# A decoder trunk on one core: split weights kept in device memory between the two halves of the tokens

## The chip, the core and the metric

The kernel runs on one core of one Trainium2 chip. The metric is device time in microseconds (us) of one execution, lower being better. The core has a matrix engine (PE, whose weight loads are listed as PEld), a vector engine (DVE), a scalar engine (ACT), a general engine (POOL), and SyncE (SP), which in this kernel issues every DMA. Each engine works through its own list of instructions in order; semaphores tie the lists together.

## The reference, cut to what matters

Two layers over 1024 tokens of width 1024. Layer 0 normalises, projects, runs a state-space mixer (S5) beside a stick-breaking attention, and projects back with `w_out`; layer 1 mixes by trailing windows. Each layer then runs a squared-ReLU MLP of width 4096 and a gated embedding:

```python
    for i in range(DEPTH):
        if i % 2 == 0:
            h = h + even_mixer(h, ln_mix_even[j], w_in_even[j], ..., w_out_even[j])
        else:
            h = h + pool_mixer(rms_norm(h, ln_mix_odd[j]), pool_w[j], pool_scale[j])
        hn = rms_norm(h, ln_mlp[i])
        h = h + jnp.square(jax.nn.relu(hn @ w_mlp_up[i])) @ w_mlp_down[i]
        gate = jax.nn.sigmoid(rms_norm(h, ln_ple[i]) @ w_ple_gate[i])
        h = h + (p[i] @ w_ple_up[i]) * gate
```

## The kernel before

**A product in three passes.** All matrices are fp32. Every operand of a large product is cut into a rounded part and a remainder (hi and lo, both fp32r), and `gemm` (L480) adds three products: hi with hi, lo with hi, hi with lo. For a weight this is done by `wload` and `split`: a DMA (L468) brings 512 KB (128 partitions x 1024 numbers) into a raw tile (tag `wr`, two buffers), ACT writes hi (L448), and DVE writes lo as raw minus hi (L452). Hi and lo are tiles of tag `wh`, eight buffers, so four pairs. In the S5 stage four of the eight hold S5 tables, in the first MLP of layer 0 four hold the hidden units; then only two pairs go round. One full weight tile feeds 24 matmuls of 128x512.

**Tokens in two halves.** A product's moving side is 512 tokens wide, so most of the program runs first for half 0 and later for half 1. Twelve tiles of `w_in` (numbered c8 to c15, then c4 to c7: keys, values, queries), four of each part of `w_out`, the first four tiles of `w_up` and of `w_down` of each layer, seven gate tiles and one `w_pu` tile of layer 0, and two tiles of `pool_w` are loaded and split once for each half: 46 tiles, twice each. The rest of the MLP is done by a seven-product scheme over both halves (`seven`), whose weights are loaded once (L882, tiles `q7`).

**What sets the order.** The source is a set of generators woven by fixed rates (`weave`): projections and `w_out` with S5 and attention, the gated embedding of layer 0 with the pooling mixer, half 0 of the next MLP with the pooling of half 1. A scheduler then lays each engine's list by priority and by when buffers come free, and adds the waits. SP's list holds, in one order, all weight loads, the loads of `x`, sets of 16 small DMAs that build S5's matrix M from `kt` (L364, four times), and the `q7` loads.

**Places that the prediction speaks of.** `put_qk` (L642) takes a projected tile out of PSUM on DVE; `s5_pass` copies `kt` on ACT (L354); `turned` copies attention weights on ACT (L735); `pool` computes windows on DVE (L1326 to L1349); `mlp` applies relu (L840), makes the hidden pair (L841 to L843) and adds into the residual (L854); `mlp_all` builds half 1's operands for the seven products on DVE (L894, L1206).

Of the kernel before, what the change touches and what calls it, by code (L numbers as in the profile page):

```python
# [11 lines left out]
F32 = mybir.dt.float32  # L12
F32R = mybir.dt.float32r
# [6 lines left out]
P = 128  # L20
# [20 lines left out]
class Kern:  # L41
    def __init__(self, ctx, tc, A):
        self.tc, self.nc, self.A = tc, tc.nc, A

        self.sb = ctx.enter_context(tc.tile_pool(name="sb", bufs=1))
        self.hi = ctx.enter_context(tc.tile_pool(name="hi", bufs=1))
        self.ps = ctx.enter_context(tc.tile_pool(name="ps", bufs=1, space=PSUM))
        self.bufs = dict(t2=3, acc=2, u=26, at=8, wq=4, r0=1, r1=1, wr=2, wh=8, mm=2, z=2, b=2, av=1, st=1)
        self.n = 0

# [410 lines left out]
            out += [(hi[:, i, :], lo[:, i, :]) for i in range(2)]  # L461
        return out

    def wload(self, src, K, tags=("wr", "wh"), hi_eng="a"):

        raw = self.t([P, 1024], tags[0], name="wr")
        hi, lo = (self.t([P, 1024], tags[1], F32R, name="w") for _ in range(2))
        self.nc.sync.dma_start(out=raw, in_=src)  # L468
        self.split(raw, hi, lo, hi_eng)
        return tuple(t.rearrange("p (k n) -> p k n", k=K) for t in (hi, lo))  # L470

    def gemm(self, ps, w, m, x, first=True, last=True, turn=0, going=False):

# [337 lines left out]
    def w_out(self, part, hf, mix, h, last=False, tag="wh"):  # L811
        for n in range(8):
            if n % 2 == 0:
                w = self.wload(self.A["w_out"][4 * part + n // 2], 4, ("wr", tag))
            ps = self.p([P, HT], "mm")
            self.gemm(ps, w, n % 2, mix)
            self.nc.vector.tensor_tensor(out=h[n], in0=h[n], in1=ps, op=ALU.add)
            if last:
                self.final(hf, n, h[n], G_MLP[0], "v")
            yield  # L820


    def mlp(self, i, f, halves, h, tag="at", up=()):

        nc, v = self.nc, self.nc.vector
        load = lambda m: self.wload(self.A["w_up"][i, 4 * f + m], 8)
        n_up = 2 if tag == "wh" else 4
        up = list(up) + [load(m) for m in range(len(up), n_up)]
        hid = {}
        for hf in halves:  # L830
            x = self.xg[hf]
            hid[hf] = self.act(4, "hid", tag)
            for m in range(4):
                ps = self.p([P, HT], "mm")
                self.gemm(ps, up[m], 0, x)
                if self.r[hf] is None:
                    self.norm_end(hf)
                hi, lo = hid[hf][m]
                t = self.t([P, HT], "t2", name="relu")
                v.scalar_tensor_tensor(out=t, in0=ps, scalar=0.0, in1=self.r[hf], op0=ALU.max, op1=ALU.mult)  # L840
                nc.scalar.activation(out=hi, in_=t, func=AF.Square)  # L841
                nc.scalar.activation(out=t, in_=t, func=AF.Square)
                v.tensor_tensor(out=lo, in0=t, in1=hi.bitcast(F32), op=ALU.subtract)  # L843
                if m + n_up < 4:
                    up.append(load(m + n_up))
                yield
        dn = None
        for hf in halves:
            for m in range(8):
                ps = self.p([P, HT], "mm")  # L850
                if m % 2 == 0:
                    dn = self.wload(self.A["w_down"][i, 4 * f + m // 2], 4)
                self.gemm(ps, dn, m % 2, hid[hf])
                v.tensor_tensor(out=h[hf][m], in0=h[hf][m], in1=ps, op=ALU.add)  # L854
                yield
# [352 lines left out]
        return x[:2], x[2:]  # L1208

    def first_up(self, i):  # L1210
        return [self.wload(self.A["w_up"][i, m], 8) for m in range(2)]

    def between(self, i, solo):

# [46 lines left out]
    def ple(self, i, halves, h):  # L1261
        nc, v = self.nc, self.nc.vector
        A = self.A
        jobs = [(m, hf) for m in range(8) for hf in halves]
        early, self.early = self.early or (None, None), None
        wu = {0: early[0] or self.wload(A["w_pu"][i, 0], 2)}
        w = {0: early[1] or self.wload(A["w_gate"][i, 0], 8)}
        ups, depth, x = [], 4, list(self.xg)

        def up(at):  # L1270
            if at < len(jobs):
                m, hf = jobs[at]
                if m // 4 not in wu:
                    wu[1] = self.wload(A["w_pu"][i, 1], 2)
                ups.append(self.p([P, HT], "zb"[at // 2 % 2]))
                self.gemm(ups[at], wu[m // 4], m % 4, self.pt[hf])

        for at in range(depth):
            up(at)
        for at, (m, hf) in enumerate(jobs):  # L1280
            if m + 1 not in w and m < 7:
                w[m + 1] = self.wload(A["w_gate"][i, m + 1], 8)
            hk = h[hf][m]
            ps = self.p([P, HT], "mm")
            self.gemm(ps, w[m], 0, x[hf], turn=4)
            if self.r[hf] is None:
                self.preload()
                self.norm_end(hf)
            sg = self.t([P, HT], "t2", name="sg")
            v.tensor_tensor(out=sg, in0=ps, in1=self.r[hf], op=ALU.mult)  # L1290
            self.last_act = nc.scalar.activation(out=sg, in_=sg, func=AF.Sigmoid)
            v.tensor_tensor(out=sg, in0=sg, in1=ups[at], op=ALU.mult)
            v.tensor_tensor(out=hk, in0=hk, in1=sg, op=ALU.add)
            up(at + depth)
            if i == 1:
                nc.sync.dma_start(out=A["out"][m, :, hf * HT:(hf + 1) * HT], in_=hk)
            else:
                self.final(hf, m, hk, G_ODD, "v", ("at", "at", "u", "u"))
            yield
        for hf in halves:  # L1300
            self.r[hf] = None


    def pool(self, hf, h):
# [7 lines left out]
        def start(m):  # L1312
            gi = m // 2
            ps = self.p([P, HT], "av")
            if m % 4 == 0:
                self.pw = self.wload(self.A["pool_w"][m // 4], 4)
            wt = [t[:, 2 * (gi % 2):2 * (gi % 2) + 2] for t in self.pw]
            self.gemm(ps, wt, m % 2, xg[2 * gi:2 * gi + 2])
            if m == 0:
                self.norm_end(hf)  # L1320
            z, nx = (self.t([P, 16 + HT], "wq", name=nm) for nm in ("pz", "win"))
            if hf == 0:
                g.memset(z[:, 0:16], 0.0)
            else:
                nc.scalar.copy(out=z[:, 0:16], in_=self.halo[:, m, :])
            v.scalar_tensor_tensor(out=z[:, 16:], in0=ps, scalar=self.gain[:, G_POOL + m:G_POOL + m + 1], in1=self.r[hf],  # L1326
                                   op0=ALU.mult, op1=ALU.mult)
            if gi == 0:
                add(v, nx[:, 16:], z[:, 16:], z[:, 15:15 + HT])
            else:  # L1330
                w = 2 << gi
                first = 0.0
                if hf == 1:
                    first = self.tail[:, m:m + 1]
                v.tensor_tensor_scan(out=nx[:, 16:], data0=z[:, 16:], data1=z[:, 16 - w:16 + HT - w], initial=first,  # L1335
                                     op0=ALU.add, op1=ALU.subtract)
            if hf == 0:
                nc.scalar.copy(out=self.halo[:, m, :], in_=z[:, HT:])
                if gi:
                    nc.scalar.copy(out=self.tail[:, m:m + 1], in_=nx[:, 15 + HT:])  # L1340
            v.tensor_tensor(out=h[m], in0=h[m], in1=z[:, 16:], op=ALU.subtract)
            win[m] = nx, z

        def finish(m):
# [5 lines left out]
            self.final(hf, m, h[m], G_MLP[1])  # L1350

        start(0)
        for m in range(8):
            if m < 7:
                start(m + 1)
            finish(m)
            yield
# [11 lines left out]
    def build(self):  # L1369
# [6 lines left out]
        s5 = chain(self.s5_params(), *(self.s5_pass(gt) for gt in range(4)))  # L1376
        self.k, self.q, self.v = [[], []], [[], []], []

        ws = self.ahead(2, [lambda c=c: self.wload(self.A["w_in"][c], 8) for _ in range(2)
                            for c in (8, 9, 10, 11, 12, 13, 14, 15, 4, 5, 6, 7)])  # L1380

        def kvq(hf):
# [42 lines left out]
        pool = self.pool(0, h[0])  # L1425
# [4 lines left out]
        pool = self.pool(1, h[1])  # L1430
# [108 lines left out]
```

## Time and profile before

| | |
|---|---|
| median of three runs | 2117.95 us (2117.68 to 2119.14) |
| the profiled execution, its own time | 2119.18 us |
| its span, first to last instruction | 2117.4 us |
| PE, DVE, ACT busy in the span | 2030.2, 1781.6, 1176.8 us |
| mean granted PE clock | 0.981 of full |
| DMA: moved, share of the 16 engines | 136.24 MB, 19.0% on the queue that SP feeds |

The span falls into stages. To about 330 us: projections with S5 woven in, then attention until 590; `w_out` of half 1 and the first MLP part of half 1 until 674; the seven products of layer 0 until about 1215; the gated embedding, the pooling mixer and layer 1's first MLP part until 1473; the seven products of layer 1 and the last gate to the end. A share of busy time is an average over all of these, so tables by stretch of time are the ones to read. A row of such a table gives, for each engine, busy microseconds and the number of instructions, then the granted clock, the share of the DMA engines and GB/s. Where a row ends in brackets, they give the idle time before the instruction and what ended it.

### The profile page before, as it was taken

The numbers are of one execution on the slowest core, as the hardware profiler recorded it, in microseconds if no ns is written. First come the engines' busy times: TensorE is split into PE (matmuls) and PEld (weight loads), VectorE is DVE, ScalarE is ACT, GpSimd is POOL, SyncE is SP. The second block draws the span as 40 slices with busy tenths as digits, with TensorE's granted clock in tenths as the row PEclk, the third lists the DMA queues.
The fourth block names the chain that finished last, engine by engine and source line by source line (L and its number), as shares of the span: only waits on it lengthen the run. The fifth ranks groups of instructions, "written<-read, shape, count | busy, mean of one in ns | idle before, by whom it ended". The sixth has DMA issues, their size and how long they took to land.

```text
span 2117.4 us, 24722 instructions
## 1 busy us (share of the span) xinstructions
PE 2030.2 (96%) x9464; PEld 1606.6 (76%) x9464; DVE 1781.6 (84%) x2339; ACT 1176.8 (56%) x1701; POOL 131.3 (6%) x263
## 2 busy tenths in 40 slices
PE   7999899999999999999999999879999999999998
PEld 5777665666677888888888887658888888888886
DVE  8876477888778798989769978988797998879999
ACT  5233478877744645555365655533654656365662
POOL 2678000000000000000000000000000000000000
PEclk9999899999999999999999999989999999999999
DMA  5121111210141210211211131231210211210221
GB/s 174 46 64 49 56 60 50 84 47 31 41 150 50 80 50 30 80 57 36 67 60 40 52 108 60 90 111 59 70 50 30 90 40 40 80 60 31 70 70 60
DMA packets 44741, 136.24 MB, mean 64 GB/s; under 512 B 9552, under 2 KB 10704, under 8 KB 44624
## 3 DMA queue, kind: packets, MB, share of 16 engines
q1 hardware_dynamic: 44624, 134.67, 19.0%
q8 instruction: 74, 1.21, 0.2%
q14 instruction: 43, 0.35, 0.1%
HBM read 129.28 MB, written 4.19 MB: 63 GB/s over the span
## 4 chain that ended last, share of the span: by engine, by line
PE 73%; DVE 18%; ACT 4%; issue 3%; DMA 1%; POOL 0%; SPq 0%; DVEq 0%; ACTq 0%
PE mm L480 26%; PE z L480 15%; PE b L480 13%; PE av L480 7%; PE st L480 7%; DVE rz L720 3%; DVE w L452 2%; DVE zs L724 1%; DVE xgl L532 1%; PE av L750 1%; DVE acc L502 1%; PE z L703 1%; ACT na L716 1%; ACT na L717 1%; DVE win L1335 1%
## 5 line engine op out<-in xcount | busy, mean ns | idle before, releaser
L480 PE MATMUL mm<-xgh,w 128*128 128x512 f32 x880 | 288.9, 405 | 6.9 <-DVE k L642 4.4
L452 DVE TENSOR_TENSOR w<-q,w 128x1024 fp32r<-128x1024 f32 x204 | 247.2, 1219 | 0.2 <-ACT w L448 0.2
L448 ACT CAST w<-q 128x1024 fp32r<-128x1024 f32 x204 | 212.7, 1047 | 35.0 <-PE mm L480 20.4
L448 ACT CAST hsh<-H 128x1024 fp32r<-128x1024 f32 x98 | 102.2, 1046 | 196.7 <-PE st L480 82.5
L480 PEld LDWEIGHTS mm<-xgh,w 128*128 128x128 f32 x880 | 167.9, 194 | 48.4 <-issue 9.7
L480 PE MATMUL z<-xsh,w 128*128 128x512 f32 x576 | 177.7, 390 | 0.0
L480 PE MATMUL mm<-xgl,w 128*128 128x512 f32 x440 | 177.0, 402 | 0.0
L448 ACT CAST w<-wr 128x1024 fp32r<-128x1024 f32 x98 | 102.3, 1047 | 126.8 <-PE mm L480 73.1
L452 DVE TENSOR_TENSOR w<-wr,w 128x1024 fp32r<-128x1024 f32 x98 | 128.9, 1322 | 28.4 <-ACT w L448 12.2
L894 DVE TENSOR_TENSOR q<-q,q 128x1024 f32<-128x1024 f32 x114 | 137.2, 1220 | 17.2 <-DMA q<-in_w_down 11.5
L480 PE MATMUL b<-xsh,w 128*128 128x512 f32 x448 | 137.9, 389 | 0.0
L480 PE MATMUL mm<-hsh,w 128*128 128x512 f32 x448 | 137.9, 389 | 0.0
L448 ACT CAST xsh<-X 128x1024 fp32r<-128x1024 f32 x72 | 75.5, 1051 | 98.2 <-PE st L480 51.2
L452 DVE TENSOR_TENSOR hsl<-H,hsh 128x1024 fp32r<-128x1024 f32 x98 | 119.5, 1220 | 10.7 <-ACT hsh L448 10.7
L480 PEld LDWEIGHTS z<-xsh,w 128*128 128x128 f32 x576 | 108.2, 188 | 22.9 <-issue 0.5
L480 PE MATMUL mm<-xsh,w 128*128 128x512 f32 x400 | 123.6, 389 | 0.0
L452 DVE TENSOR_TENSOR xsl<-X,xsh 128x1024 fp32r<-128x1024 f32 x72 | 87.4, 1222 | 40.9 <-ACT xsh L448 40.5
L480 PE MATMUL z<-xsl,w 128*128 128x512 f32 x288 | 112.1, 389 | 0.0
L720 DVE TENSOR_TENSOR_SCAN rz<-na,rz 128x128 f32<-128x128 f32 (+7 forms) x64 | 84.7, 1347 | 27.0 <-ACT na L717 27.0
L480 PE MATMUL mm<-hidh,w 128*128 128x512 f32 x256 | 89.2, 425 | 18.0 <-DVE w L452 9.4
L452 DVE TENSOR_TENSOR xsl<-xt,xsh 128x512 fp32r<-128x512 f32 x108 | 70.1, 686 | 42.0 <-ACT xsh L448 41.9
L480 PE MATMUL b<-hsh,w 128*128 128x512 f32 x336 | 103.6, 389 | 0.0
(366 smaller groups left out, 4842.9 us busy)
## 6 DMA issues: line engine op xcount, KB each, us to landing
q<-in_w_up SPq DMA_DIRECT2D x56, 512.0 KB, 3.8
q<-in_w_down SPq DMA_DIRECT2D x56, 512.0 KB, 3.6
wr<-in_w_in SPq DMA_DIRECT2D x26, 512.0 KB, 3.6
wr<-in_w_out SPq DMA_DIRECT2D x16, 512.0 KB, 3.5
wr<-in_w_up SPq DMA_DIRECT2D x16, 512.0 KB, 3.5
wr<-in_w_down SPq DMA_DIRECT2D x16, 512.0 KB, 3.5
x<-in_x SPq DMA_DIRECT2D x15, 512.0 KB, 4.8
wr<-in_w_gate SPq DMA_DIRECT2D x15, 512.0 KB, 3.4
```

The source lines that it names most:

```text
L448: nc.scalar.copy(out=hi, in_=src)
L452: e.tensor_tensor(out=lo, in0=src, in1=hi.bitcast(F32), op=ALU.subtract)
L480: self.nc.tensor.matmul(ps, a, b, start=(first and n == 0 and i == 0), stop=(last and n == K - 1 and i == 2), skip_group_check=going)
L502: e.tensor_tensor(out=self.acc[hf], in0=self.acc[hf], in1=sq, op=ALU.add)
L532: self.nc.vector.scalar_tensor_tensor(out=lo, in0=x, scalar=g, in1=hi.bitcast(F32), op0=ALU.mult, op1=ALU.subtract)
L703: nc.tensor.matmul(pz[:, 0:b1 - b0], self.q[hf][pair // 2][rows, pair % 2, i * P:(i + 1) * P], self.k[b0 // HT][pair // 2][rows, pair % 2, ...
L716: nc.scalar.activation(out=na, in_=na, func=AF.Exp)
L717: nc.scalar.activation(out=na, in_=na, func=AF.Ln, bias=1.0)
L720: v.tensor_tensor_scan(out=rz[:, rev], data0=na[:, rev], data1=rz[:, rev], initial=0.0, op0=ALU.add, op1=ALU.add)
L724: v.tensor_tensor(out=zs, in0=zs, in1=rz, op=ALU.subtract)
L750: nc.tensor.matmul(self.avp[64 * o:64 * o + 64, i * P:(i + 1) * P], self.v[kb // 4 * 2 + pair // 2][:, kb % 4, cs], w[:, at * P:(at + 1) * ...
L894: (self.nc.vector if eng == "v" else self.nc.gpsimd).tensor_tensor(out=o, in0=a, in1=b, op=op)
```

## The change

`wload` gets a name for each of the 46 tiles that both halves use. On the first call it works as before and then stores hi and lo, 512 KB each, into two buffers of device memory. On the second call there is no raw tile and no split: two DMAs bring hi and lo straight into `wh` tiles (for half 1 of `w_out`, part 1, into tiles of tag `wq`).

```diff
-    def wload(self, src, K, tags=("wr", "wh"), hi_eng="a"):
-
-        raw = self.t([P, 1024], tags[0], name="wr")
-        hi, lo = (self.t([P, 1024], tags[1], F32R, name="w") for _ in range(2))
-        self.nc.sync.dma_start(out=raw, in_=src)
-        self.split(raw, hi, lo, hi_eng)
-        return tuple(t.rearrange("p (k n) -> p k n", k=K) for t in (hi, lo))
+    def wload(self, src, K, tags=("wr", "wh"), keep=None):
+
+        if keep in self.kept:
+            parts = [self.t([P, 1024], tags[1], F32R, name="w") for _ in range(2)]
+            for t, d in zip(parts, self.kept[keep]):
+                self.nc.sync.dma_start(out=t.bitcast(F32), in_=d)
+        else:
+            raw = self.t([P, 1024], tags[0], name="wr")
+            parts = [self.t([P, 1024], tags[1], F32R, name="w") for _ in range(2)]
+            self.nc.sync.dma_start(out=raw, in_=src)
+            self.split(raw, *parts)
+            if keep is not None:
+                self.kept[keep] = []
+                for t, e in zip(parts, "hl"):
+                    name = "_".join(str(x) for x in keep) + e
+                    d = self.dr.tile([P, 1024], F32, tag=name, name=name, bufs=1)
+                    self.nc.sync.dma_start(out=d, in_=t.bitcast(F32))
+                    self.kept[keep].append(d)
+        return tuple(t.rearrange("p (k n) -> p k n", k=K) for t in parts)
...
-                w = self.wload(self.A["w_out"][4 * part + n // 2], 4, ("wr", tag))
+                w = self.wload(self.A["w_out"][4 * part + n // 2], 4, ("wr", tag), ("out", part, n // 2))
...
-        load = lambda m: self.wload(self.A["w_up"][i, 4 * f + m], 8)
+        load = lambda m: self.wload(self.A["w_up"][i, 4 * f + m], 8, keep=("up", i, m))
...
-                    dn = self.wload(self.A["w_down"][i, 4 * f + m // 2], 4)
+                    dn = self.wload(self.A["w_down"][i, 4 * f + m // 2], 4, keep=("down", i, m // 2))
...
-                    wu[1] = self.wload(A["w_pu"][i, 1], 2)
+                    wu[1] = self.wload(A["w_pu"][i, 1], 2, keep=("pu", 1))
...
-                w[m + 1] = self.wload(A["w_gate"][i, m + 1], 8)
+                w[m + 1] = self.wload(A["w_gate"][i, m + 1], 8, keep=("gate", m + 1))
...
-                self.pw = self.wload(self.A["pool_w"][m // 4], 4)
+                self.pw = self.wload(self.A["pool_w"][m // 4], 4, keep=("pool", m // 4))
...
-        ws = self.ahead(2, [lambda c=c: self.wload(self.A["w_in"][c], 8) for _ in range(2)
+        ws = self.ahead(2, [lambda c=c: self.wload(self.A["w_in"][c], 8, keep=("in", c)) for _ in range(2)
```

SP's list grows from 301 to 439 rows: 46 raw loads go, 92 stores and 92 loads come. DVE's list shrinks from 2267 to 2217 rows and ACT's from 1694 to 1647. Since the scheduler lays the lists anew, the rest moves a little too. Three places.

SP in the S5 stage, in half 1's projections. `wr` are raw tiles, `w` split ones, `in_9h` and `in_9l` the kept parts of c9, `M_279` (now `M_275`) the S5 matrix of the last of four passes. Before:

```order
L468 DMA wr_267_1902<-in_w_in 128x1024
L468 DMA wr_284_2050<-in_w_in 128x1024
L468 DMA wr_307_2195<-in_w_in 128x1024
L468 DMA wr_323_2264<-in_w_in 128x1024
L468 DMA wr_343_2351<-in_w_in 128x1024
L364 DMA M_279_2018<-kt_277_2003 16x4x128 x2
```

Now:

```order
L472 DMA w_239_1788<-in_9h_597 128x1024
L472 DMA w_240_1789<-in_9l_599 128x1024
L472 DMA w_251_1858<-in_10h_716 128x1024
L472 DMA w_252_1859<-in_10l_718 128x1024
L472 DMA w_264_1946<-in_11h_783 128x1024
L472 DMA w_265_1947<-in_11l_785 128x1024
L472 DMA w_280_2092<-in_12h_926 128x1024
L472 DMA w_281_2093<-in_12l_928 128x1024
L472 DMA w_302_2235<-in_13h_1006 128x1024
L472 DMA w_303_2236<-in_13l_1008 128x1024
L367 DMA M_275_2060<-kt_273_2045 16x4x128 x2
```

The five raw loads ahead of M (c11 to c15) waited for a free raw tile; the ten loads that stand there now (c9 to c13) wait for split tiles that PE has finished with, and M stands behind them. The set of M before it follows the loads of c8 in the same way.

SP at the start of half 1's MLP part in layer 0 (`in_w_up` is the weight in its input layout, `up_0_0h` the kept first tile). Before:

```order
L468 DMA wr_914_5309<-in_w_up 128x1024
L468 DMA wr_917_5315<-in_w_up 128x1024
L882 DMA q7_921_5335<-in_w_up 128x1024
L882 DMA q7_922_5337<-in_w_up 128x1024
L882 DMA q7_923_5339<-in_w_up 128x1024
L882 DMA q7_924_5341<-in_w_up 128x1024
L468 DMA wr_925_5343<-in_w_up 128x1024
```

Now:

```order
L472 DMA w_880_5293<-out_1_3h_3665 128x1024
L472 DMA w_881_5294<-out_1_3l_3667 128x1024
L897 DMA q7_899_5405<-in_w_up 128x1024
L897 DMA q7_900_5407<-in_w_up 128x1024
L897 DMA q7_901_5409<-in_w_up 128x1024
L897 DMA q7_902_5411<-in_w_up 128x1024
L472 DMA w_894_5383<-up_0_0h_4597 128x1024
L472 DMA w_895_5384<-up_0_0l_4599 128x1024
```

The first two `up` tiles were fetched ahead of four `q7` tiles; now they come behind them.

DVE in layer 1, behind the pooling mixer of half 1. `ra` and `r1` belong to the norm of half 1, `X` are operands of the seven products, `x` are residual rows. Before, with w_1927 the split of the second `up` tile for half 1 and w_1931 that of the fourth `down` tile for half 0:

```order
L894 TENSOR_TENSOR X_1951_11286<-X_1951_11286,r0_1846_10759 128x1024
L894 TENSOR_TENSOR X_1952_11289<-xgh_1758_10295,xgl_1759_10296 128x1024
L511 SCALAR_TENSOR_TENSOR ra_1920_11135<-st_1918_11132,ra_1920_11135 128x512
L854 TENSOR_TENSOR x_529_3311<-x_529_3311,mm_1921_11142 128x512
L512 TENSOR_SCALAR ra_1920_11135<-ra_1920_11135 128x512
L452 TENSOR_TENSOR w_1927_11164<-wr_1925_11162,w_1926_11163 128x1024
L513 TENSOR_TENSOR r1_1919_11134<-r1_1919_11134,ra_1920_11135 128x512
L452 TENSOR_TENSOR w_1931_11171<-wr_1929_11169,w_1930_11170 128x1024
```

Now, with w_1891 the split of that fourth `down` tile:

```order
L909 TENSOR_TENSOR X_1910_11391<-xgh_1727_10383,xgl_1728_10384 128x1024
L869 TENSOR_TENSOR x_517_3337<-x_517_3337,mm_1876_11214 128x512
L909 TENSOR_TENSOR X_1909_11388<-X_1909_11388,r0_1810_10857 128x1024
L909 TENSOR_TENSOR X_1910_11391<-X_1910_11391,r0_1810_10857 128x1024
L526 SCALAR_TENSOR_TENSOR ra_1882_11241<-st_1880_11238,ra_1882_11241 128x512
L869 TENSOR_TENSOR x_517_3337<-x_517_3337,mm_1883_11248 128x512
L527 TENSOR_SCALAR ra_1882_11241<-ra_1882_11241 128x512
L455 TENSOR_TENSOR w_1891_11273<-wr_1889_11271,w_1890_11272 128x1024
```

The split for half 1 is gone and the fourth `down` tile's split stands ahead of the end of the norm. (Line numbers of the changed kernel are 3 larger than before in the class's head and 15 larger behind `wload`.)

More of the change, by code (lines that the diff above doesn't have):

```diff
@@ L47, in __init__ @@
         self.ps = ctx.enter_context(tc.tile_pool(name="ps", bufs=1, space=PSUM))
+        self.dr = ctx.enter_context(tc.tile_pool(name="dr", bufs=1, space=bass.MemoryType.DRAM))
+        self.kept = {}
         self.bufs = dict(t2=3, acc=2, u=26, at=8, wq=4, r0=1, r1=1, wr=2, wh=8, mm=2, z=2, b=2, av=1, st=1)
@@ L1210, in first_up @@
     def first_up(self, i):
-        return [self.wload(self.A["w_up"][i, m], 8) for m in range(2)]
+        return [self.wload(self.A["w_up"][i, m], 8, keep=("up", i, m)) for m in range(2)]
     def between(self, i, solo):
```

## The prediction

> **What bounds the kernel now.** I read the busy times first, then a stretch at full rate, then the stretches in which the 46 second uses lie.
>
> ```profile
> PE 2030.2 (96%) x9464; PEld 1606.6 (76%) x9464; DVE 1781.6 (84%) x2339; ACT 1176.8 (56%) x1701; POOL 131.3 (6%) x263
> ...
> q1 hardware_dynamic: 44624, 134.67, 19.0%
> ```
>
> PE sets the time, and the change takes no matmul away. It can only give back what PE loses between matmuls. In this table the columns are stretch, length, busy time and count of PE, PEld, DVE, ACT, POOL, then the granted clock, the DMA share and GB/s.
>
> ```profile
> 700.00:800.00 100.00, 100.00 (x443) 82.79 (x442) 84.09 (x94) 53.92 (x73) 0.00 (x0) 1.00 0.23 75
> ...
> 165.00:330.00 165.00, 152.69 (x847) 109.27 (x846) 110.11 (x162) 91.21 (x150) 41.47 (x83) 0.93 0.18 55
> 330.00:580.00 250.00, 234.30 (x1360) 160.93 (x1360) 206.48 (x240) 202.15 (x327) 0.00 (x0) 0.99 0.15 51
> 580.00:675.00 95.00, 89.42 (x409) 72.19 (x408) 80.28 (x98) 40.79 (x54) 0.00 (x0) 0.96 0.32 111
> 1240.00:1290.00 50.00, 50.00 (x219) 40.59 (x218) 37.15 (x49) 29.69 (x39) 0.00 (x0) 1.00 0.29 95
> 1290.00:1350.00 60.00, 52.36 (x212) 40.18 (x211) 59.52 (x92) 33.25 (x58) 0.67 (x6) 0.94 0.19 62
> 1350.00:1410.00 60.00, 48.59 (x172) 34.89 (x171) 54.05 (x77) 26.14 (x46) 0.00 (x0) 0.88 0.28 92
> 1410.00:1456.00 46.00, 41.51 (x162) 32.38 (x161) 39.53 (x46) 16.78 (x21) 0.00 (x0) 0.90 0.35 120
> ```
>
> At full rate PE does 443 matmuls in 100 us. By that rate the last three stretches lose 60 x 4.43 - 212 = 54 matmuls (12.1 us), 94 (21.2 us) and 42 (9.4 us). The first two hold matmuls of other sizes, so there I take idle time: 12.3 and 15.7 us. The third is idle for 5.6 us and runs at 0.96, another 95 x 0.04 = 3.8, so 9.4 us. These losses are the most that any edit there can return. Only in 1290 to 1350 is DVE the limit all the time: 59.52 of 60.
>
> **What is removed.** Each second use drops a cast on ACT, a subtract on DVE and a raw load:
>
> ```profile
> L448 ACT CAST w<-wr x98: 1022/1047/1098, 13.9 to 1452.6; 128x1024 fp32r<-128x1024 f32 x98
> L452 DVE TENSOR_TENSOR w<-wr,w x98: 1185/1219/5735, 19.4 to 1453.7; 128x1024 fp32r<-128x1024 f32 x98
> L468 SPq DMA_DIRECT2D wr<-in_w_in x26: 327/328/528, 10.3 to 266.3; - x26
> ```
>
> That is 46 x 1.22 = 56 us of DVE and 48 us of ACT in all (minimum, median, maximum in ns). Counted by the order of the program's loads, of the 46 there lie 12 in 165 to 330, 4 in 330 to 580, 12 in 580 to 675, and 4, 4, 3 and 7 in the four stretches of layer 1. The value depends on what waits behind each.
>
> *165 to 330.* One split stands out.
>
> ```profile
> 208.03 5.74 DVE L452 TENSOR_TENSOR w<-wr,w 128x1024 fp32r<-128x1024 f32 x1 [5.95 <-ACT Y L440]
> 213.68 0.68 DVE L642 TENSOR_TENSOR k<-mm,r 128x512 f32<-128x512 f32 x1
> ...
> 215.54 1.12 PE L370 MATMUL z<-ident,vs 128*128 128x128 f32 x4 [4.24 <-ACT kt L354]
> ```
>
> It took 5.74 us while POOL built S5 tables, and k, then the copy of `kt`, then PE stood behind it. It goes, so I take 4 of PE's 4.24 us. Bounds 0 (another DVE instruction is held there in its place) and the 12.3 that the stretch loses. The Trainium skill, "SBUF — State Buffer", section "Who interferes with whom", says that a DVE instruction with two SBUF inputs contends with a GpSimd instruction that reads SBUF; the trace agrees (5.74 against 1.22 us), and k's first input is in PSUM, so by that rule the 4 comes back whole.
>
> *330 to 580.* Attention; 4 removed. DVE has 43 us of slack there, so I take 1; bounds 0 and 4 x 1.22 = 4.9.
>
> *580 to 675.* 12 of the 14 splits go.
>
> ```profile
> 586.06 1.04 ACT L448 CAST w<-wr 128x1024 fp32r<-128x1024 f32 x1 [2.63 <-DMA wr<-in_w_out]
> 587.64 1.53 PE L750 MATMUL av<-na,v 128*64 128x128 f32 x24 [1.15 <-ACT na L735]
> ...
> 650.35 0.79 PE L480 MATMUL mm<-hidh,w 128*128 128x512 f32 x1 [3.50 <-DVE w L452]
> ```
>
> At 650 PE waits 3.50 us for the split of the first `down` tile, which stands behind the operands of the seven products on DVE. At 587 PE waits 1.15 us for a copy of attention weights, behind a cast that had waited 2.63 us for its raw tile. Both go: 4.65, and 1.35 for the clock after them, so 6. Bounds 0 and 9.4.
>
> *1240 to 1290.* PE is busy for all 50 us: 0.
>
> *1290 to 1410.* 4 + 3 splits on an engine that is the limit: 4 x 1.22 = 5, then 3 x 1.22 = 3.7, of which I take 3, since DVE has 6 us of slack there. Sum 8. Bounds 0 and 12.1 + 21.2 = 33, if the clock recovers as well, as these two rows allow:
>
> ```profile
> 1311.31 0.70 PE L480 MATMUL mm<-xgh,w 128*128 128x512 f32 x2 [1.90 <-DVE sg L1290]
> ...
> 1326.30 1.22 PE L480 MATMUL av<-xgh,w 128*128 128x512 f32 x2 [4.48 <-DVE pz L1326]
> ```
>
> Two matmuls take 0.70 us after 1.90 us of idling and 1.22 after 4.48: a long wait costs again behind itself. The waits here, though, end with `sg` and `pz`, results of long chains that the change leaves.
>
> *1410 to 1456.* 7 of 8 splits go.
>
> ```profile
> 1408.21 0.33 SPq L468 DMA_DIRECT2D wr<-in_w_down  x1
> ...
> 1415.49 0.39 PE L480 MATMUL mm<-hidl,w 128*128 128x512 f32 x1
> 1417.27 0.89 PE L480 MATMUL mm<-hidh,w 128*128 128x512 f32 x2 [1.39 <-ACT w L448]
> 1420.87 0.80 PE L480 MATMUL mm<-hidh,w 128*128 128x512 f32 x1 [2.71 <-DVE w L452]
> 1421.46 0.63 PE L480 MATMUL mm<-hidl,w 128*128 128x512 f32 x1
> ```
>
> PE waits 1.39 and 2.71 us for the fourth `down` tile of half 0. Its cast and split stand behind those of a second `up` tile for half 1, which go. Behind them one matmul takes 0.63 us where it took 0.39 ahead of them; nine matmuls at that price are 2 us more, so 4.1 + 2 = 6. Bounds 0 and 9.4.
>
> Removals sum to 4 + 1 + 6 + 0 + 8 + 6 = 25 us.
>
> **What is added on SP.** 92 stores and 92 loads come, 46 loads go: 138 x 0.33 = 45 us of issuing on a list of 2117 us, hidden unless they stand ahead of something urgent. By the queue's row 134.67 MB took 19.0% of 2117 us, 2.99 us per MB; 48 MB of stores (92 x 0.524) and 24 of loads more than before add 72 x 2.99 = 215 us, 10% of the span, in stretches with a share of 0.15 to 0.35. The bandwidth is hidden.
>
> **The new wait.** A raw load waits only for a raw tile, which the split frees early. A read needs a `wh` pair, which PE frees only when it has done with a tile, and it holds up all that stands behind it on SP. From release to use, before: cast and split, 1.05 + 1.22 = 2.27 us. Now: two issues and a landing.
>
> ```profile
> wr<-in_w_up SPq DMA_DIRECT2D x3, 512.0 KB, 4.9
> ...
> 674.12 5.44 PE z L480 x24
> ```
>
> With the 4.9 us of the busy stretch 1400 to 1425 that is 0.33 + 4.9 = 5.2 for hi, 5.6 for lo. With two pairs PE has one tile's work as cover: 24 matmuls, 5.44 us, more where other matmuls are woven in. A read on time just fits. Not on time are those behind other things:
>
> ```profile
> 215.94 11.11 SPq L364 DMA_DIRECT2D M<-kt  x16
> ...
> 223.82 0.69 DVE L642 TENSOR_TENSOR k<-mm,r 128x512 f32<-128x512 f32 x1 [8.09 <-PE mm L480]
> ...
> 235.57 0.38 PE L426 MATMUL z<-M,U 128*128 128x128 f32 x2
> ...
> 608.72 6.57 SPq L882 DMA_DIRECT2D q<-in_w_up  x4
> ...
> 619.43 20.68 PE mm L480 x91
> ...
> M<-kt SPq DMA_DIRECT2D x4, 16.0 KB, 1.8
> ```
>
> M now stands behind c13, whose pair is free when c11 is done (PE's last matmul for it ends before 223.8): 223.8 + 0.66 + 11.1 = 235.6, and 1.8 for the landing of its last and smallest transfers (the last row), so 237.4 where PE wants it at 235.57: 1.8 late. `up` 0 of half 1 stands behind four `q7` loads, whose issues end at 608.72 + 6.57 = 615.29 and wait for tiles of their own; 615.29 + 0.33 + 4.9 = 620.5 for hi, against 619.43 where PE begins with it (the fifth row, from the chain of waits), and a little more for lo: 2. The last two tiles of `w_out` for half 1, in `wq` pairs: 1. Among the 14 reads of layer 1, between `q7` loads and stores: 3. Sum 2 + 2 + 1 + 3 = 8. Bounds: 0, and 30 if every fourth read is late by 2.6, half of hi's 5.2 (46 / 4 x 2.6).
> **The sum.** 2119.18 - 25 + 8 = 2102 for a run such as the profiled one; the median is 1.2 lower: **2101 us**.
>
> **The rivals.** *All gain:* the reads are on time and the clock recovers behind the waits that go: 25 + 8 for the clock of 1290 to 1410 (a quarter of 33) and no cost, 2118 - 33 = 2085. For it: reads stand far ahead on SP's list. Against: two pairs and 5.44 us of cover. *Nothing:* PE waits at the next producer of the same chain (`sg`, `pz`, the relu of the next tile), and the few late reads take the rest: half of the 25 is lost again and the reads of layer 1 cost 6 in place of 3: 2118 - 12 + 11 = 2117. For it: the waits of 1290 to 1410 end with such chains. Against: the waits at 215, 650 and 1420 name the split itself or what stands right behind it. *Slower:* SP blocks. One read that waits for its pair holds the stores, raw loads, M and `q7` behind it, and these are then late for their own users. It decides once the mean lateness over 46 reads is above 25 / 46 = 0.54 us. With every second tile late by 1.6 us (between M's 1.8 above and the 1.4 by which a landing grows below), 23 x 1.6 = 37, 12 more than the gain: 2130. For it: M behind ten waiting loads, `up` behind four `q7`. Against: most of the 46 have woven work beside them, and a calm landing is shorter than the 4.9 above:
>
> ```profile
> wr<-in_w_out SPq DMA_DIRECT2D x16, 512.0 KB, 3.5
> ```
>
> From calm to busy a landing grows by 1.4 us. The Trainium skill, "DMA: Bandwidth & Descriptors", section "Latency and other measured facts", gives HBM access as 0.2 us on average and 2 us at high load, so by it the added traffic could itself make reads late, by up to 1.8 us each, 46 x 1.8 = 83 as an estimate from that page; the rows above bear out no more than 1.4, and only where the share is high.
>
> That the change doesn't do what it says is excluded: DVE's list has 52 weight splits where it had 98.
>
> **Chances.** Mine 0.55, all gain 0.13, nothing 0.13, slower 0.19. Its own range is 2090 to 2113 (31 less 3, and 16 less 11). To hold 8 in 10 I go from 2084, just under the second case, to 2121, past the third, leaving out the slower one. A measurement of this kernel tells 0.2%, 4.2 us, from no change: faster than 2113.7 are my case and the second, 0.67 (a point of mine lost); within, 0.14; slower 0.19.
>
> **What would show it.** Right: no wait of PE at the copy of `kt` near 215; none for a weight split where half 1's `down` part starts, nor at half 0's fourth `down` tile; DVE below 59 of 60 in the stretch of the gated embedding, with PE's count up by the same share. The cost: PE or PEld idle until a DMA of a kept part (`in`, `out`, `up`, `down`, `gate`, `pool`) or of M, some 8 us in all. Wrong upward: tens of us of such waits, and SP idle until PE in most of them. Wrong downward: none, and a clock of 0.95 or more in 1350 to 1410.

## The result and the profile after

The changed kernel takes 2098.78 us, median of six runs (2093.93 to 2103.36), against 2118.14 us for six runs of the kernel before (2115.79 to 2119.14). The ratio is 0.9903, with a 95% interval of 0.9888 to 0.9919: 17 to 24 us faster. The forecast was 2101 with a range of 2084 to 2121. The profiled execution took 2099.48 us.

The page of the changed kernel, the two rows that answer to those of before:

```profile
PE 2022.6 (96%) x9464; PEld 1604.6 (76%) x9464; DVE 1740.9 (83%) x2293; ACT 1131.3 (54%) x1655; POOL 125.9 (6%) x263
...
q1 hardware_dynamic: 64496, 207.03, 28.1%
```

DVE is busy for 41 us less and ACT for 46; the queue moves 72 MB more. The prediction had 56 us for DVE's 46 splits, so the rest of its list takes 15 us longer. PE's busy time falls by 8 us with the same matmuls, at a mean granted clock of 0.984 where it was 0.981.

Where the 20 us of span went is read from landmarks, instructions that stand in both kernels. Of before, an attention product at the end of the S5 stage (the one of 64x384) and the start of layer 1's seven products (that of layer 0's, at 674.12, is shown above):

```profile
313.01 1.18 PE L703 MATMUL z<-k,q 64*128 64x384 f32 x4 [1.30 <-ACT zs L708]
...
1473.56 5.44 PE z L480 x24
```

The same three of the changed kernel, from its timeline and its chain of waits:

```profile
314.79 1.18 PE L718 MATMUL z<-k,q 64*128 64x384 f32 x4 [0.79 <-ACT zs L723]
...
667.19 5.44 PE z L495 x24
...
1454.03 5.44 PE z L495 x24
```

The differences of these starts cut each profiled execution into stretches. The kernels with a name of their own are those of the experiments below:

| us | start to S5's end | to layer 0's seven products | to layer 1's seven products |
|---|---|---|---|
| before | 313.0 | 361.1 | 799.4 |
| the change | 314.8 | 352.4 | 786.8 |
| the change, second profile | 316.9 | 352.6 | 787.0 |
| no w_in | 312.4 | 352.6 | 786.3 |
| w_in only | 316.2 | 359.3 | 799.0 |
| stores only | 317.9 | 358.6 | 800.9 |
| layer 0 only | 317.4 | 354.0 | 799.4 |
| layer 1 only | 317.4 | 360.6 | 784.7 |
| low part only | 316.0 | 350.7 | 794.8 |
| high part only | 314.7 | 359.8 | 797.2 |
| gate and pool only | 318.1 | 360.7 | 796.2 |
| layer 1's up and down only | 314.2 | 359.1 | 799.1 |
| w_in's reads on ACT's queue | 308.6 | 350.8 | 787.9 |

The rest of the program takes 643.5 to 645 us in all of them. So the change gained nothing up to the end of S5, 8.7 us to the first seven products, and 12.6 to the second. A row is one execution: kernels that do the same work in a stretch still lie up to 2 us apart in the second column, and 5 in the first, where the clock varies (last section). In three stretches of the changed kernel, the last from the relu that opens half 0's MLP part to layer 1's seven products, with the columns of the tables above:

```profile
165.00:330.00 165.00, 155.85 (x902) 112.32 (x898) 110.81 (x156) 82.37 (x143) 47.59 (x104) 0.97 0.35 122
...
580.00:675.00 95.00, 94.69 (x444) 77.38 (x443) 71.01 (x89) 31.96 (x45) 0.00 (x0) 1.00 0.50 183
...
1345.87:1454.03 108.16, 95.45 (x387) 74.40 (x388) 92.45 (x121) 34.61 (x56) 0.00 (x0) 0.95 0.53 189
```

From 580 to 675 PE now runs 444 matmuls at full clock, where it ran 409. The DMA share has gone from 0.32 to 0.50 there, and PE waits for none of it. PE's waits for a DMA of M or of a kept part, in the whole program (sum, times, longest):

```profile
PE z L429 <- DMA M<-kt: 1.8, 2, 1.6
PE mm L495 <- DMA w<-in_9h: 1.7, 1, 1.7
...
PE mm L495 <- DMA w<-in_9l: 0.6, 1, 0.6
```

All of them are in the S5 stage. The new wait that the prediction priced at 8 us is 4.1 us there, and nothing elsewhere.

### The profile page after: what moved, and what is told of

It reads as the page before. It is cut to its first block, busy times and chain, and to the rows that moved or that the text cites. A ratio compares the mean times of both kernels' runs of the same rounds, so it can differ in the third digit from the quotient of the medians.

```text
span 2097.7 us, 24863 instructions
## 1 busy us (share of the span) xinstructions
PE 2022.6 (96%) x9464; PEld 1604.6 (76%) x9464; DVE 1740.9 (83%) x2293; ACT 1131.3 (54%) x1655; POOL 125.9 (6%) x263
## 4 chain that ended last, share of the span: by engine, by line
PE 76%; DVE 16%; ACT 4%; issue 2%; DMA 1%; SPq 1%; POOL 0%; DVEq 0%; ACTq 0%
PE mm L495 28%; PE z L495 15%; PE b L495 13%; PE av L495 7%; PE st L495 7%; DVE rz L735 2%; PE av L765 1%; DVE zs L739 1%; PE z L718 1%; DVE xgl L547 1%; DVE acc L517 1%; DVE w L455 1%; ACT na L731 1%; PE z L432 1%; PE b L749 1%
## 5 line engine op out<-in xcount | busy, mean ns | idle before, releaser
L495 PE MATMUL mm<-xgh,w 128*128 128x512 f32 x880 | 286.7, 404 | 11.4 <-DVE k L657 4.4
L495 PE MATMUL z<-hsh,w 128*128 128x512 f32 x336 | 103.4, 389 | 0.0
L495 PEld LDWEIGHTS mm<-xgl,w 128*128 128x128 f32 x440 | 84.6, 192 | 18.3 <-issue 0.8
L495 PEld LDWEIGHTS b<-xsh,w 128*128 128x128 f32 x448 | 84.1, 188 | 17.5
```

Source lines behind the costliest of these rows:

```text
L495: self.nc.tensor.matmul(ps, a, b, start=(first and n == 0 and i == 0), stop=(last and n == K - 1 and i == 2), skip_group_check=going)
```

## The experiments

Each kernel is timed beside the kernel before on the same chip; the medians of before were 2119.98, 2119.98 and 2120.02 us for the three groups of four. A kernel's own times spread by 5 to 17 us, so the ratios carry the verdicts, and profiles say where.

**Stores only.** The second use is as before:

```diff
-        if keep in self.kept:
+        again = keep in self.kept
+        if False:
...
-            if keep is not None:
+            if keep is not None and not again:
                 self.kept[keep] = []
```

> All 46 tiles are stored in the first half, as in the change, but the second half loads and splits them as before; nothing is read back. Mine: the stores are hidden, 2118 within 3 us. Rival: the stores' entries on SP delay the raw loads behind them; then PE's new wait of 3.1 us for rq near 116 us, and the half clock behind it, stand here too, and the time is 3 to 8 us above before.

Measured: 2123.55 us, ratio 1.0022 (1.0011 to 1.0034), 2 to 7 us slower. The rival's time was right. The timeline has the wait it named, and in the ten microseconds behind it the clock is at half:

```profile
117.79 0.50 PE L681 MATMUL b<-rq,selT 4*128 4x512 f32 x2 [3.12 <-DVE rq L676]
...
120.00:130.00 10.00, 10.00 (x40) 7.00 (x39) 7.21 (x5) 0.59 (x1) 10.00 (x35) 0.50 0.44 159
```

The cause that the rival named, late raw loads, is not what stands ahead of this wait. What differs there is the order on DVE: before, a weight split stood ahead of the chain that makes `rq`; with the stores the scheduler puts that split behind it. DVE then begins the chain's first steps earlier, which lets POOL begin its S5 tables 2 us earlier, beside the end of the chain. The same two steps of the norm, before and in the change:

```profile
110.17 0.42 DVE L512 TENSOR_SCALAR ra<-ra 128x512 f32<-128x512 f32 x1
...
111.10 0.68 DVE L513 TENSOR_TENSOR rq<-rq,ra 128x512 f32<-128x512 f32 x1
```

```profile
111.61 1.28 DVE L527 TENSOR_SCALAR ra<-ra 128x512 f32<-128x512 f32 x1
112.92 1.63 DVE L528 TENSOR_TENSOR rq<-rq,ra 128x512 f32<-128x512 f32 x1
...
116.28 0.79 PE L680 MATMUL b<-rq,selT 4*128 4x512 f32 x2 [3.10 <-DVE rq L675]
```

They take 1.28 and 1.63 us in place of 0.42 and 0.68, and PE waits 3.10 us. That the order is the cause, and that POOL's tables are what slows these steps, is argued from the timelines, not tried.

**Only w_in.** Here and in the next kernels one condition picks the tiles that are kept:

```diff
+        if keep is not None and not (keep[0] == "in"):
+            keep = None
         if keep in self.kept:
```

> Only the 12 tiles of w_in are kept and read back. Mine, by the two traces: the S5 stage gave the change nothing (its lag went from -0.4 to +1.8 us between 109 and 313 us), so 2119 to 2121. Rival, as I predicted it: the split of c12 that held PE for 4.2 us goes and M is late by 2, so 2116 or less.

Measured: 2121.45 us, ratio 1.0008 (0.9993 to 1.0024): no gain, as the traces had said, and not the 2 us that the prediction had. This is the sum of a loss and a gain, which the section on the prediction takes apart.

**Only layer 0's w_out, up and down tiles** (`keep[0] == "out"`, or up and down with `keep[1] == 0`).

> Only w_out and layer 0's up and down tiles are kept. Mine: the stretch from 313 to 674 us gave 8.7 us, so 2118 - 9 = 2109. Rival: what the change gained there came from work that the w_in part had shifted; then this alone gives 0 to 4.

Measured: 2109.99 us, ratio 0.9956 (0.9935 to 0.9978): 10 us, within 5 to 14. The table above has 354.0 for its stretch, 7.1 us less than before where the change has 8.7, and nothing for layer 1. (The profiled execution, 2116.45 us, is the slowest of five; it lost 4.4 us in the S5 stage.)

**Only layer 1's tiles and the gate** (gate, pu, pool, or up and down with `keep[1] == 1`).

> Only gate, pu, pool and layer 1's up and down tiles are kept. Mine: the stretch from 1279 to 1473 us gave 12.6 us, so 2105.5. Rival: 0 to 5, if the chains behind sg and pz hold PE anyway once nothing earlier has moved.

Measured: 2108.53 us, ratio 0.9946 (0.9929 to 0.9963): 11.4 us. With the 10 of layer 0 and the -1.5 of w_in that is 20, the whole gain. The three parts add up.

**Without w_in** (`keep[0] != "in"`), and **the change once more** beside it.

> The change without its w_in part: 34 tiles kept. Mine: the stores of w_in alone bring the wait of 3.1 us near 116 us and its half clock, the reads of w_in the waits of 195 to 200 us, and both are paid back only in part; so this beats the change by 2 us or a little more: 2096 to 2099 where the change is at 2099. No wait of PE for a DMA of M or of a kept part before 330 us. Rival: the parts help each other and this loses 2 or more against the change.

> The change itself on the same chip as the kernels beside it, for the comparison and as a second profile: 2099, 2094 to 2104. If the stretch near 116 us shows the wait of 3.1 us for rq here too, it belongs to the order of the work and not to one execution.

Measured: 2099.03 us, ratio 0.9898 (0.9875 to 0.9920), without w_in, and 2100.59 us, 0.9898 (0.9873 to 0.9924), for the change. They can't be told apart. The twelve tiles of w_in, a quarter of the 46, bring nothing on the whole. Without them PE waits for no kept part and for no M at all; with them the wait of 3.1 us and those of 195 to 200 us are there in both profiles of the change.

**Only the remainder kept, only the rounded part kept.** Both leave w_in out. Half 1 loads the raw tile; one part is read back, the other made again:

```diff
+        again = keep in self.kept
+        raw = self.t([P, 1024], tags[0], name="wr")
...
+        self.nc.sync.dma_start(out=raw, in_=src)
+        if again:
+            self.nc.sync.dma_start(out=parts[1].bitcast(F32), in_=self.kept[keep])
+            self.nc.scalar.copy(out=parts[0], in_=raw)
```

(With the rounded part, `parts[0]` is read and DVE subtracts.)

> 34 tiles without w_in; only the remainder (lo) is kept: half 1 loads the raw tile, ACT casts it to hi again, lo is read back. DVE is relieved, ACT is not. Mine: the waits at 650 and 1420 us and the limit of 1290 to 1350 us are DVE's, so 15 to 18 of the 21 us stay: 2100 to 2105. Rival: ACT's cast and the raw load are half of it: 2108.

> 34 tiles without w_in; only the rounded part (hi) is kept: half 1 loads the raw tile, reads hi back, and DVE subtracts as before. ACT is relieved, DVE is not. Mine: 2 to 5 us below before, 2114 to 2118. Rival: 2108, if the cast on the way to the subtract was what was late.

Measured: 2106.48 us, ratio 0.9933 (0.9911 to 0.9956), with the remainder, and 2120.14 us, 1.0003 (0.9985 to 1.0020), with the rounded part. Relieving ACT alone is worth nothing, relieving DVE alone 13.5 of 21, less than the 15 to 18 that were expected. By the table the gain of layer 0 is wholly DVE's (350.7 us with the remainder kept, 359.8 with the rounded part). In layer 1 only 4.6 of the 12.6 to 13 stay. The reason is at the fourth `down` tile of half 0, in the kernel with the remainder kept:

```profile
1398.66 0.43 SPq L474 DMA_DIRECT2D wr<-in_w_down  x1
```

```profile
1406.41 0.73 PE L495 MATMUL mm<-hidh,w 128*128 128x512 f32 x2 [1.51 <-ACT w L451]
1410.19 0.79 PE L495 MATMUL mm<-hidh,w 128*128 128x512 f32 x1 [3.05 <-DVE w L455]
```

and in the changed kernel:

```profile
1365.45 0.64 SPq L476 DMA_DIRECT2D wr<-in_w_down  x1
```

The raw load of that tile stood at 1408.21 before, behind raw loads of half 1's `up` tiles, for there are two raw tiles. The change takes those away and the load goes out 43 us earlier, 36 when counted from layer 0's seven products; with raw loads kept it comes at 1398.66 and the waits of 1.4 and 2.7 us stay. So here the raw tile seems to count as much as the subtract; no run frees the one without the other.

**Gate and pool only, layer 1's up and down only**, the two halves of the layer 1 part.

> Only the seven gate tiles, the w_pu tile and the two pool tiles are kept. Mine: DVE's limit in 1290 to 1350 us is relieved by 10 splits, 6 us below before (the prediction's term for 1240 to 1410 was 8, with the first up tile). Rival: the chains behind sg and pz or the raw tiles of the up and down loads hold PE anyway: 0 to 3.

> Only layer 1's four up and four down tiles are kept. Mine: the waits of 1.4 and 2.7 us for half 0's fourth down tile shrink and the clock recovers: 6 us below before, so that this and the kernel with gate and pool kept add up to the 11 to 13 of layer 1. Rival: nothing by itself, 0 to 2, the gain of layer 1 needs both.

Measured: 2117.51 us, ratio 0.9987 (0.9970 to 1.0004), and 2124.01 us, 1.0014 (0.9994 to 1.0034). My sum fell: neither is told from no change, and together, in the kernel with layer 1 only, they give 11.4. From the relu that opens half 0's MLP part to layer 1's seven products, before, gate and pool only, up and down only, and both:

```profile
1358.95:1473.56 114.61, 100.47 (x382) 77.08 (x382) 101.39 (x129) 42.29 (x64) 0.00 (x0) 0.90 0.25 86
```

```profile
1359.29:1475.04 115.75, 100.96 (x381) 77.91 (x382) 100.33 (x128) 41.57 (x63) 0.00 (x0) 0.88 0.26 89
```

```profile
1357.12:1472.30 115.18, 102.80 (x387) 79.31 (x388) 94.89 (x123) 36.34 (x58) 0.00 (x0) 0.88 0.47 171
```

```profile
1356.71:1462.70 105.99, 93.44 (x387) 73.16 (x388) 92.44 (x121) 34.58 (x56) 0.00 (x0) 0.97 0.54 193
```

From layer 0's seven products to that relu the four take 684.8, 680.5, 683.9 and 678.7 us, so ahead of it the two halves nearly add (4.4 and 0.9, together 6.1). Behind it they don't. Up and down only and both have the same idle time there, 12.4 and 12.6 us; what differs is the clock, 0.88 against 0.97, some 10 us of 115. With up and down only PE waits there in several pieces, with both in one long piece:

```profile
1391.94 0.79 PE L497 MATMUL mm<-hidh,w 128*128 128x512 f32 x1 [2.58 <-DVE x L871]
1397.38 0.80 PE L497 MATMUL mm<-hidh,w 128*128 128x512 f32 x1 [1.85 <-DVE w L455]
...
1408.60 0.79 PE L497 MATMUL mm<-hidh,w 128*128 128x512 f32 x1 [2.36 <-DVE x L871]
```

```profile
1401.68 0.79 PE L497 MATMUL mm<-hidh,w 128*128 128x512 f32 x1 [6.91 <-DVE x L871]
```

Behind each of these waits the next matmul takes 0.79 or 0.80 us, where one at full clock takes 0.39, so many pieces pay for it many times. That this makes the 10 us is argued, from one execution of each, and why the order falls so is not settled; that the halves don't add is shown by the times.

**Each part read twice**, without w_in.

```diff
             for t, d in zip(parts, self.kept[keep]):
-                self.nc.sync.dma_start(out=t.bitcast(F32), in_=d)
+                for _ in range(2):
+                    self.nc.sync.dma_start(out=t.bitcast(F32), in_=d)
```

> 34 tiles without w_in, each part read back twice into the same tile, one read behind the other; the matmuls wait for the second. The traffic of the reads and their time to landing grow. Mine: a read now has 0.5 to 1 us to spare where only two pairs go round (a landing of 4.1 us and 0.4 of issuing in 5.44 us of cover), so two more transfers make some 16 tiles late by 1.5 to 2 us each: 20 to 35 us slower than the same kernel with single reads, 2120 to 2135, with PE waiting for DMAs of kept parts. Rival: the cover is far larger than one tile's matmuls: under 5 us.

Measured: 2129.48 us, ratio 1.0048 (1.0028 to 1.0069): 30 us slower than with single reads, as expected. PE now waits for kept parts, and the stretch from 580 to 675 is idle for 10 us:

```profile
PE mm L498 <- DMA w<-up_0l: 3.6, 1, 3.6
PE mm L498 <- DMA w<-out_2l: 1.2, 1, 1.2
PE mm L498 <- DMA w<-down_1l: 1.0, 1, 1.0
```

```profile
580.00:675.00 95.00, 84.85 (x366) 65.48 (x365) 62.31 (x80) 23.98 (x36) 0.00 (x0) 0.96 0.82 291
```

So the cover is real and thin: one more 512 KB for each part turns a gain of 21 us into a loss of 9. The profiled execution, 2119.20 us, is the fastest of ten, 10 us below the median, and PE's waits for kept parts add up to 7.3 us in it, so most of the 30 is not traced; nor does this run part the time of the transfers from the place they take on SP.

**w_in's reads on ACT's queue.**

```diff
-                self.nc.sync.dma_start(out=t.bitcast(F32), in_=d)
+                (self.nc.scalar if keep[0] == "in" else self.nc.sync).dma_start(out=t.bitcast(F32), in_=d)
```

> The change, with the reads of w_in alone issued on ACT's queue, so that they don't stand behind M's sixteen DMAs on SP, nor M behind them. Mine: PE's waits for M and for c9 at 195 to 200 us go (4.1 us in the change), the wait near 116 us stays; 1 to 4 us below the change. Rival: ACT stands still while a read waits for its pair, and its casts and copies come late: 3 us or more above the change.

Measured: 2093.41 us (2090.80 to 2095.52), ratio 0.9874 (0.9849 to 0.9899): the fastest of all, 5 to 7 us below the two medians of the change, though the intervals overlap a little. PE waits for no M and no kept part, and the clock of the S5 stage is 1.00:

```profile
165.00:330.00 165.00, 157.55 (x954) 113.10 (x953) 111.35 (x165) 86.10 (x155) 48.41 (x104) 1.00 0.37 122
```

The S5 stage ends at 308.6 us, 6.2 earlier than in the change. The wait near 116 is still there, as expected:

```profile
116.08 0.79 PE L680 MATMUL b<-rq,selT 4*128 4x512 f32 x2 [3.10 <-DVE rq L675]
```

## Why the prediction was right, and where its steps were off

The time, the sign and the two large terms were right: 2101 forecast, 2098.8 measured. Some of the agreement is luck of opposite errors: the S5 stage was to gain 2 us (4 less 2 for M) and lost 1.8, layer 0 gave 4.7 more than forecast, layer 1 1.6 more.

**165 to 330: the term of 4 came, and the stage lost it ahead of that.** The split of c12 that took 5.74 us went, and so did the wait for the copy of `kt` at 215. A product of S5's third pass, which PE reaches with the same work behind it in both kernels, cuts the stage in two. Before, and in the change:

```profile
177.09 2.02 PE L396 MATMUL z<-U,VT 128*64 128x128 f32 x32
```

```profile
186.96 2.02 PE L399 MATMUL z<-U,VT 128*64 128x128 f32 x32
```

The change comes there 9.9 us late. From there to S5's end it takes 127.8 us, where before takes 135.9. The other kernels say how much of either is the change:

| us | start to this product | this product to S5's end |
|---|---|---|
| before | 177.1 | 135.9 |
| eight that don't keep w_in | 179.7 to 182.2 | 131.3 to 136.0 |
| stores only | 186.6 | 131.3 |
| w_in read back on SP, three profiles | 186.7 to 187.2 | 127.8 to 130.2 |
| w_in read back on ACT's queue | 187.8 | 120.8 |

So storing w_in costs 4 to 10 us near 116 us, by the wait for `rq` and the half clock behind it, and reading it back gains 1 to 8 us later, with the new waits of 4.1 us already paid. My upper bound of 12.3 us was idle time alone; the clock of 0.93 there was worth about 11 more (0.07 of PE's 152.69 us), and with the reads on ACT's queue, at a clock of 1.00, this part is 15 us shorter than before. (That kernel has 7 of these matmuls, some 2 us, ahead of the product and not behind it.)

My bound at nothing, "another DVE instruction is held there in its place", happened too, in the pass before, to the step that makes `kt` itself. Before, and in the change:

```profile
167.42 0.21 DVE L358 TENSOR_TENSOR kt<-kt,s5blk 32x64 f32<-32x64 f32 x1 [0.32 <-ACT kt L354]
```

```profile
176.92 6.66 DVE L361 TENSOR_TENSOR kt<-kt,s5blk 32x64 f32<-32x64 f32 x1 [1.82 <-ACT kt L357]
...
183.61 11.38 SPq L367 DMA_DIRECT2D M<-kt  x16
195.09 0.53 SPq L472 DMA_DIRECT2D w<-in_9h  x1
```

```profile
195.65 0.46 PE L429 MATMUL z<-M,U 128*128 128x128 f32 x2 [1.60 <-DMA M<-kt]
...
198.48 0.80 PE L495 MATMUL mm<-xgh,w 128*128 128x512 f32 x1 [1.73 <-DMA w<-in_9h]
```

An instruction of 32x64 took 6.66 us beside POOL's tables. M's DMAs waited for it on SP, and c9's read stood behind M. The rule of the Trainium skill that I cited, "SBUF — State Buffer", section "Who interferes with whom", agrees again, but not my use of it: here the contention didn't leave with the split, it came upon another instruction with two SBUF inputs.

**The cost of M: right in size, by luck.** I had M 1.8 us late behind c13's read, in the last pass, and there PE doesn't wait for it. In the third pass M was 1.8 us late through `kt`, and the read was late behind M. With those reads on ACT's queue c9's goes out 13 us earlier, and PE's list has c9's matmuls ahead of M's product:

```profile
182.09 0.33 ACTq L472 DMA_DIRECT2D w<-in_9h  x1
```

```profile
198.59 0.60 PE L429 MATMUL z<-M,U 128*128 128x128 f32 x4
```

Both waits are gone (2093.4), so the order on SP made the read late. M itself is not earlier: `kt` takes 6.67 us there too and M's issues end at 194.2; PE only comes to it later.

**The stores: priced at nothing, cost 2 to 7 us.** "Hidden unless they stand ahead of something urgent" was argued by bandwidth and issuing. Alone they cost 4.7 us by the ratio, through the wait near 116 us. In the change this is paid back, and no w_in and all w_in are the same.

**330 to 580 and 580 to 675: 1 + 6, less 3: forecast 4, measured 8.7** (10 alone). The waits of 1.15 and 3.50 us went and the clock came back, as said. From the first matmul of half 1's `down` part to the seven products, before and in the change, the same 98 matmuls:

```profile
645.37:674.12 28.75, 24.67 (x98) 19.60 (x97) 25.39 (x29) 9.66 (x11) 0.00 (x0) 0.88 0.22 74
```

```profile
645.21:667.19 21.98, 21.98 (x98) 18.13 (x97) 16.27 (x20) 5.68 (x7) 0.00 (x0) 1.00 0.13 48
```

These are 6.8 of the 8.7 us, 4.1 of idle time and 2.7 by the clock; I had 1.35 for the clock. Both costs were nothing. That of `up` 0 was a misreading: I took 619.43 in the chain of waits as the tile's first matmul, but that row merges all products of one helper, and the timeline of before has half 0's `down` tile there. The tile begins here, 4 us later:

```profile
623.61 0.62 PE L480 MATMUL mm<-xgh,w 128*128 128x512 f32 x2
```

In the change its read, and the landing of lo, which is issued at 617.32:

```profile
616.95 0.33 SPq L472 DMA_DIRECT2D w<-up_0h  x1
```

```profile
w<-up_0l SPq DMA_DIRECT2D x1, 512.0 KB, 5.2
```

So lo is there at 622.5, about 1 us ahead of its use, and reading twice makes it 3.6 us late. My 620.5 for hi was good; what it was held against was not.

**Layer 1: 8 + 6, less 3: forecast 11, measured 12.6** (11.4 alone). From layer 0's seven products up to the relu of half 0's MLP part the change takes 6.1 us less, and 6.4 behind it, near the sum. But I added one term for splits on a busy DVE and one for the fourth `down` tile as if each stood alone, and each alone gives nothing that can be measured. Nor did the waits for that tile go, as I had said; they fell from 1.39 and 2.71 us to

```profile
1400.95 0.89 PE L495 MATMUL mm<-hidh,w 128*128 128x512 f32 x2 [0.59 <-ACT w L451]
...
1402.81 0.77 PE L495 MATMUL mm<-hidh,w 128*128 128x512 f32 x1 [0.97 <-DVE w L455]
```

No matmul waits for one of layer 1's reads; those of up and down take 3.1 to 6.6 us to land, more in part than the 5.44 us of one tile that I held against them.

**The rivals.** "All gain" fails by its price of nothing: the waits for reads and M cost 4.1 us, and the stores more. "Nothing", a gain that passes to the next producer, is what each half of layer 1 shows alone, and the whole does not. "Slower", late reads on SP, is a real mechanism: it is what the S5 stage shows once, and reading twice brings out more of it. It didn't decide, since the mean lateness over 46 reads was 4.1 / 46 = 0.09 us, far below 0.54. The second rule of the Trainium skill that I cited, "DMA: Bandwidth & Descriptors", section "Latency and other measured facts", spoke of latency that grows under load. Landings of parts did grow, up to 9.0 us (the last of eight reads issued from 622 to 630 us), but where the reads went out ahead of their use.

## What to carry to other kernels

Here, work taken off the engine that feeds a stage paid at the few waits that ended on it, and again by the clock behind them; work taken off an engine beside it paid nothing. A read that replaces a recomputation must be held against the time between the release of its buffer and the first use, read off the timeline at the first matmul of that tile and not off a merged row, and against what stands ahead of it in its queue. Try each group of tiles alone before adding terms: here a quarter of them brought nothing, and two halves that brought nothing apart brought 11 us together. And where a group brings nothing, cut its stage in two before writing that it does nothing: here a loss and a gain of some microseconds each lay in it.

## What the runs showed of the hardware

The clock can fall with little idle time. Two executions have the same instructions at the same times until 116 us: before, and the kernel with layer 0 only, whose program is the same up to there.

```profile
113.90 0.50 PE L665 MATMUL b<-rq,selT 4*128 4x512 f32 x2 [0.35 <-DVE rq L660]
...
118.53 0.71 PE L429 MATMUL z<-ca,X 64*128 64x128 f32 x8
```

```profile
113.90 0.50 PE L682 MATMUL b<-rq,selT 4*128 4x512 f32 x2 [0.35 <-DVE rq L677]
...
120.10 1.23 PE L432 MATMUL z<-ca,X 64*128 64x128 f32 x8
```

Both wait 0.35 us there and 1.2 at 109, and yet in the second the matmuls from about 116.4 to 127 take the time of half clock, which costs 4.5 us. In the ten microseconds from 120 the clock lay between 0.63 and 1.00 in nine profiled executions without the wait of 3.1 us, and was 0.50 in all five with it. The matmuls there are short ones of few rows. "TensorE: Matmul & The Clock Gate" of the Trainium skill, Part 1, speaks of a free-running window of activity, which fits the chance in it; its table names an idle window of about 3.4 us as what lowers the clock, and here the longest wait near was 1.2 us. What did lower it is not shown. This chance is worth a quarter of the change's gain, and is likely a good part of the spread of 15 us that the kernel before shows (2109.98 to 2125.36).
